# Linear attention on one core: K and V in 8 KB rows over eight heads, a new order of the work, and stores of 2 MB

## The chip, the core and the metric

The kernel runs on one core of a Trainium2 chip. The metric is the time of one execution on the device, in microseconds (us). Of the kernel before, three runs are on record: 126.47, 126.68 and 126.68 us, median 126.68.

## What is computed

Q, K and V have the shape (8, 12, 512, 64) in fp32: 96 heads of 512 rows with 64 columns.

```
Q_feat = max(0, Q) + 1
K_feat = max(0, K) + 1
KV     = K_feat^T V            per head, 64 x 64
K_sum  = sum over rows of K_feat
out    = (Q_feat KV) / (Q_feat K_sum + 1e-10)
```

Each input has 12.58 MB, and so has the output: 50.3 MB cross between HBM and SBUF. Both kernels compute max(x + 1, 1) for the features and leave out the 1e-10.

## The kernel before, in words

**Tiling.** Rows lie on 128 partitions. K and V are loaded with 16 rows (4 KB) to a partition, so a tile of 128 partitions is four heads, 32 partitions to a head. Q is loaded with 32 rows (8 KB) to a partition, the output is stored with 8 rows (2 KB). The work goes in 12 groups g of eight heads (NG = 12). Groups 2s and 2s+1 share their loads: one of K, one of V, one of Q for sixteen heads, 2.1 MB of fp32 each. These go out from GpSimd's queue (POOL) and are cast to bf16 on the way (`load`, L106; `load_q`, L112). The first K alone comes through SP's queue, in fp32 (L93).

**A group.** DVE makes the features of K (`k_features`, two operations at L137). The V rows of each head are copied into their own 64 columns of a wide tile, `v_all` (`v_blocks`): block b holds partitions 32b to 32b+31, in columns 64b to 64b+63, the rest is zero since the start, and four more columns hold ones, one for each head, for K_sum. DVE copies three of the four blocks (L155), ACT the fourth (L153). The first matmul (`keys_values`, L171) multiplies 64 feature columns by 260 columns of `v_all`, 16 for each of two tiles n; n = 0 writes PSUM partitions 0 to 63, n = 1 writes 64 to 127. ACT copies the result into `kva` (L181, L182). Q's features (L137) are transposed on PE (L192, 16 a group) into PSUM, and copied out (L195, mostly ACT). The second matmul (L205) gives numerators and denominators in PSUM, eight matmuls for each of four parts of a group; DVE makes the reciprocal (L222) and the product (L223), called a norm here. `store` writes 1 MB a group (L126, POOL); the last two groups are stored from SP (L129, L132).

**Buffers.** The input pool has two buffers of each tensor, so the loads of pair s+2 wait until the work on pair s has read them. The second matmul's PSUM tiles have two buffers: a part's matmuls wait for the norm two parts back.

**Order.** `tc.manual_schedule()` keeps each engine's instructions in the order in which the program names them, and every engine executes its queue in order. The main loop (L265 to L281) runs over groups:

```
for g in range(last - 1):
    if g % 2:
        transposes(g - 1)
    k_features(g)
    v_blocks(g)
    if g >= 2:
        output(g - 2)
    ...
    keys_values(g)
```

So the output of a group comes two groups after its first matmul. Stores come three groups late (LAG), from POOL, behind the loads of a later pair. The last two groups are written out by hand (L282 to L301).

Of the kernel before, what the change touches and what calls it, by code (L numbers as in the profile page):

```python
# [9 lines left out]
BF16 = mybir.dt.bfloat16  # L10
ALU = mybir.AluOpType

BANK = 512
IN_BUFS = 2
OUT_BUFS = 3
LAG = 3
# [3 lines left out]
def kernel(  # L20
# [10 lines left out]

# [4 lines left out]
    C = 8  # L44
    C2 = 2 * C
    C4 = 4 * C
    R = 4
    NPAIR = B * H * S // (P * C)
    NP = 4
    NG = NPAIR // NP  # L50
# [5 lines left out]

    q_eights = view(Q, C4)
    k_dram = view(K, C2)
    v_dram = view(V, C2)
# [3 lines left out]
    head_pool = ctx.enter_context(tc.tile_pool(name="head_pool", bufs=1))  # L63
    in_pool = ctx.enter_context(tc.tile_pool(name="in_pool", bufs=IN_BUFS))
    kf_pool = ctx.enter_context(tc.tile_pool(name="kf_pool", bufs=2))
    qf_pool = ctx.enter_context(tc.tile_pool(name="qf_pool", bufs=3))
# [8 lines left out]
    NV = 4  # L75
    v_all = const.tile([P, 2, 2, C2, 4 * D1], BF16, name="v_all")
    ones = const.tile([P, 4], BF16, name="ones")
    zero = const.tile([P, 1], FP32, name="zero")
    kva_all = const.tile([P, NV, 4, 2, D1], BF16, name="kva_all")
    kva_diag = [kva_all[:, i] for i in range(NV)]  # L80

    drams = dict(k=k_dram, v=v_dram)
    raw = {}
    bufs = {}
# [4 lines left out]
    cells_of = {}  # L89

    def load_first_k():
        k_raw = head_pool.tile([P, 2, C2, D], FP32, name="k_first")
        nc.sync.dma_start(out=k_raw, in_=k_dram[:, 0:4:2])  # L93
        raw["k", 0] = k_raw

    def load(x, groups):
        s = groups[0] // 2
        if groups[0] % 2 == 0 or (x, s) not in bufs:
            bufs[x, s] = in_pool.tile([P, 4, C2, D], BF16, name=f"{x}_raw")
        if len(groups) == 2:  # L100
            ms = slice(0, 4)
            of = slice(4 * s, 4 * s + 4)
        else:
            ms = slice(groups[0] % 2, 4, 2)
            of = slice(4 * s + groups[0] % 2, 4 * s + 4, 2)
        nc.gpsimd.dma_start(out=bufs[x, s][:, ms], in_=drams[x][:, of])  # L106
        for g in groups:
            raw[x, g] = bufs[x, s][:, g % 2 : 4 : 2]

    def load_q(s):  # L110
        t = in_pool.tile([P, 2, C4, D], BF16, name="q_raw")
        nc.gpsimd.dma_start(out=t, in_=q_eights[:, 2 * s : 2 * s + 2])  # L112
        rows = t.rearrange("p n (r c) d -> p n r c d", c=C)
        for e in range(2):
            raw["q", 2 * s + e] = rows[:, :, :, 4 * e : 4 * e + 4]

    def load_pair(s):
        load("k", (2 * s, 2 * s + 1))
        load("v", (2 * s, 2 * s + 1))
        load_q(s)  # L120

    def store(g):
        s = g // 2
        o_to = o_dram[:, 2 * NP * s : 2 * NP * s + 2 * NP]
        if g < NG - 2:
            nc.gpsimd.dma_start(out=o_to[:, g % 2 : 2 * NP : 2], in_=outs[s][:, g % 2 : 2 * NP : 2])  # L126
            return
        if g == NG - 2:
            nc.sync.dma_start(out=o_to[:, 0 : 2 * NP : 2], in_=outs[s][:, 0 : 2 * NP : 2])  # L129
            return  # L130
        for h in range(2):
            nc.sync.dma_start(  # L132
                out=o_to[:, 2 * h + g % 2 : 2 * NP : NP], in_=outs[s][:, 2 * h + g % 2 : 2 * NP : NP]
            )

    def feature(dst, src):
        nc.vector.tensor_scalar(  # L137
            out=dst, in0=src, scalar1=1.0, scalar2=1.0, op0=ALU.add, op1=ALU.max
        )

    def k_features(g):
        k_raw = raw.pop(("k", g))
        kf = kf_pool.tile([P, C2, 2, D], BF16, name="kf")
        for n in range(2):
            feature(kf[:, :, n], k_raw[:, n])
        kfs[g] = kf

    def v_blocks(g):
        v_raw = raw.pop(("v", g))
        for b in range(4):  # L150
            ps = slice(32 * b, 32 * b + 32)
            if b == 3:
                nc.scalar.copy(out=v_all[ps, g % 2, :, :, b * D : b * D + D], in_=v_raw[ps])  # L153
            else:
                nc.vector.tensor_copy(  # L155
                    out=v_all[ps, g % 2, :, :, b * D : b * D + D], in_=v_raw[ps]
                )

    def q_features(g):
        q_raw = raw.pop(("q", g))  # L160
        qf = qf_pool.tile([P, R, C // 2, 2, D], BF16, name="qf")
        for n in range(2):
            feature(qf[:, :, :, n], q_raw[:, n])
        qfs[g] = qf

    def keys_values(g):
        kf = kfs.pop(g)
        kva_ps = psum_kva.tile([P, 4 * D1], FP32, name="kva_ps")
        for c in range(C2):
            for n in range(2):  # L170
                nc.tensor.matmul(  # L171
                    kva_ps[64 * n : 64 * n + 64],
                    lhsT=kf[:, c, n, :],
                    rhs=v_all[:, g % 2, n, c, :],
                    start=(c == 0),
                    stop=(c == C2 - 1),
                )
        kva = kva_diag[g % NV]
        for n in range(2):
            ps = slice(64 * n, 64 * n + 64)  # L180
            nc.scalar.copy(out=kva[ps, :, n, 0:D], in_=kva_ps[ps, 0 : 4 * D].rearrange("p (b d) -> p b d", b=4))  # L181
            nc.scalar.copy(out=kva[ps, :, n, D], in_=kva_ps[ps, 4 * D : 4 * D1])  # L182

    def transposes(g):
        qf = qfs.pop(g)
        if g % 2 == 0:
            qts[g // 2] = mid_pool.tile([P, C, P, R], BF16, name="qt")
        for half in range(2):
            qt_ps = psum_qt.tile([P, 2, R, P], BF16, name="qt_ps")
            for c in range(2):  # L190
                for r in range(R):
                    nc.tensor.transpose(qt_ps[:, c, r], qf[:, r, 2 * half + c, :, :], identity)  # L192
            copy = nc.vector.tensor_copy if half and g == NG - 2 else nc.scalar.copy
            lo = g % 2 * 4 + 2 * half
            copy(out=qts[g // 2][:, lo : lo + 2], in_=qt_ps.rearrange("p c r q -> p c q r"))  # L195

    def out_matmuls(g, h):
        qt = qts[g // 2]
        kva = kva_diag[(g // 2 * 2 + h) % NV]
        ops = [psum.tile([P, 2, BANK], FP32, tag="ps", name="o_ps") for _ in range(2)]  # L200
        for c in range(C):
            for j in range(2):
                b = 2 * (g % 2) + j
                q = 16 * (4 * h + b)
                nc.tensor.matmul(  # L205
                    ops[c // 4][64 * j : 64 * j + 64, c // 2 % 2, (c % 2) * W : (c % 2) * W + W],
                    lhsT=qt[:, c, q : q + 16, :],
                    rhs=kva[:, b],
                    start=True,
                    stop=True,  # L210
                )
        cells_of[g, h] = ops

    def norms(g, h):
        ops = cells_of.pop((g, h))
        if (g % 2, h) == (0, 0):
            outs[g // 2] = out_pool.tile([P, 2 * NP, C, D], FP32, name="o_sb")
        o_sb = outs[g // 2]
        for i in range(2):
            cells = ops[i][:, :, 0 : 2 * W].rearrange("p b (c n x) -> p b c n x", n=2, x=D1)  # L220
            recip = recip_pool.tile([P, 2, 2, 2, 1], FP32, name="recip")
            nc.vector.reciprocal(out=recip, in_=cells[:, :, :, :, D:D1])  # L222
            nc.vector.tensor_tensor(  # L223
                out=o_sb[:, 2 * h + g % 2 : 2 * NP : NP, 4 * i : 4 * i + 4].rearrange(
                    "p n (b c) d -> p b c n d", b=2
                ),
                in0=cells[:, :, :, :, 0:D],
                in1=recip.to_broadcast([P, 2, 2, 2, D]),
                op=ALU.mult,
            )  # L230

    def output(g):
        for h in range(2):
            out_matmuls(g, h)
            norms(g, h)

    def clear(i):
        t = v_all[:, i].rearrange("p n c x -> p (n c x)").bitcast(FP32)
        w = t.shape[1] * 5 // 8
        nc.vector.memset(t[:, 0:w], 0.0)  # L240
        nc.scalar.copy(out=t[:, w:], in_=zero.to_broadcast([P, t.shape[1] - w]))  # L241
        nc.vector.tensor_copy(
            out=v_all[:, i, :, :, 4 * D : 4 * D1].rearrange("p n c j -> p (n c) j"),
            in_=ones[:, None, :].to_broadcast([P, 2 * C2, 4]),
        )

    with tc.manual_schedule():
        nc.vector.memset(zero, 0.0)
        load_first_k()
        load("v", (0,))  # L250
        load_q(0)
        load("k", (1,))
# [6 lines left out]
        for t in kva_diag:  # L259
            for b in range(4):  # L260
                nc.gpsimd.memset(t[:, b], 0.0)  # L261
# [70 lines left out]
```

## Time and profile before

| | us |
|---|---|
| median of three runs | 126.68 |
| span of the profiled execution, first to last instruction | 124.7 |
| DVE busy | 89.3 (72%) |
| PE busy | 61.8 (50%) |
| ACT busy | 59.6 (48%) |
| POOL busy | 26.1 (21%) |
| mean granted PE clock | 0.847 of full speed |

The profile is of one execution with a span of 124.7 us; its own time beside the span is not recorded, and the three runs lie within 0.21 us of each other. HBM read 37.75 MB and wrote 12.58 MB, 404 GB/s over the span. A load cast from fp32 to bf16 is counted in the slices by the bytes that it writes, half of those that it reads. Matmuls overlap, so a busy time of PE or the mean of one matmul is not its cost; a burst in the timeline, its length by its count, is nearer to that. "PEld" is the weight load.

### The profile page before, as it was taken

How to read it: one execution, taken by the hardware profiler on the slowest of the kernel's cores; microseconds unless marked ns; L12 is line 12 of the kernel's file. 1: busy time of each engine (PE TensorE's matmuls, PEld its weight loads, DVE VectorE, ACT ScalarE, POOL GpSimd, SP SyncE). 2: the span in 40 equal slices, each digit the busy share in tenths (PEclk: the TensorE clock that was granted, in tenths of full speed). 3: DMA queues.
4: the chain of work that ended last, by engine and by line, in shares of the span. 5: the costliest groups of instructions: out<-in, count | busy, mean ns of one | idle time of the engine just before them, and what ended most of it. 6: DMA issues, size and time to landing. Idle time of an engine off the chain costs nothing.

```text
span 124.7 us, 2348 instructions
## 1 busy us (share of the span) xinstructions
PE 61.8 (50%) x960; PEld 50.7 (41%) x960; DVE 89.3 (72%) x191; ACT 59.6 (48%) x86; POOL 26.1 (21%) x51
## 2 busy tenths in 40 slices
PE   0004945200692838539684691069495267775300
PEld 0003735200581827428573490058384155663100
DVE  4895444206999899997999930699959699969700
ACT  7532289306039781956639462601993295450000
POOL 6991023100011630233302420302020200020000
PEclk9999999955589999995999689756999958997555
DMA  3999999999999999999999999999999999999993
GB/s 95 330 214 214 209 198 210 210 214 213 208 213 213 216 214 208 212 213 217 230 405 327 210 212 214 215 338 403 227 212 215 218 255 415 420 413 416 406 409 126
DMA packets 11803, 32.13 MB, mean 258 GB/s; under 512 B 528, under 2 KB 528, under 8 KB 11792
## 3 DMA queue, kind: packets, MB, share of 16 engines
q0 software_dynamic: 10448, 28.84, 97.4%
q1 hardware_dynamic: 1344, 3.15, 6.7%
q8 instruction: 7, 0.11, 0.3%
q14 instruction: 4, 0.03, 0.1%
HBM read 37.75 MB, written 12.58 MB: 404 GB/s over the span
## 4 chain that ended last, share of the span: by engine, by line
DMA 56%; DVE 19%; PE 8%; ACT 6%; issue 3%; POOL 2%; POOLq 0%
DMA v_raw<-in_V_dram 30%; DMA q_raw<-in_Q_dram 26%; DVE o_sb L223 8%; PE kva_ps L171 5%; DVE v_all L155 5%; ACT v_all L153 3%; DVE qf L137 2%; PE qt_ps L192 2%; DVE recip L222 2%; ACT qt L195 2%; POOL v_raw L106 1%; DVE qt L195 1%; ACT kva_all L181 1%; POOL k_raw L106 1%; DVE kf L137 1%
## 5 line engine op out<-in xcount | busy, mean ns | idle before, releaser
L205 PE MATMUL o_ps<-kva_all,qt 128*64 128x130 bf16 x384 | 20.0, 240 | 37.0 <-DVE recip L222 27.0
L171 PE MATMUL kva_ps<-v_all,kf 128*64 128x260 bf16 x384 | 29.8, 320 | 15.8 <-DVE v_all L155 15.6
L155 DVE COPY v_all<-v_raw 32x2048 bf16<-32x2048 bf16 x36 | 25.8, 717 | 13.5 <-DMA v_raw<-in_V_dram 13.1
L223 DVE TENSOR_TENSOR o_sb<-o_ps,recip 128x512 f32<-128x512 f32 x48 | 33.2, 692 | 1.6
L171 PEld LDWEIGHTS <-kf 128*64 128x64 bf16 x384 | 24.6, 130 | 19.0 <-DVE v_all L155 16.0
L205 PEld LDWEIGHTS <-qt 128*64 128x64 bf16 x384 | 14.0, 118 | 42.2 <-issue 26.0
L153 ACT COPY v_all<-v_raw 32x2048 bf16<-32x2048 bf16 x12 | 22.6, 1893 | 16.9 <-DMA v_raw<-in_V_dram 16.7
L195 ACT COPY qt<-qt_ps 128x1024 bf16<-128x1024 bf16 x23 | 22.2, 1015 | 6.8 <-PE qt_ps L192 6.5
L181 ACT CAST kva_all<-kva_ps 64x256 bf16<-64x256 f32 x24 | 8.9, 371 | 27.5 <-PE kva_ps L171 27.3
L126 POOL DMA_DIRECT2D out_dram<-o_sb x10 | 8.6, 864 | 35.9 <-DVE o_sb L223 27.2
L192 PE MATMUL qt_ps<-identity,qf 128*128 128x128 bf16 x192 | 14.8, 235 | 2.0 <-ACT qt L195 1.3
L192 PEld LDWEIGHTS <-qf 128*128 128x128 bf16 x192 | 12.4, 106 | 4.5 <-issue 2.5
L137 DVE TENSOR_SCALAR kf<-k_raw 128x1024 bf16<-128x1024 bf16 x22 | 8.5, 426 | 7.6 <-DMA k_raw<-in_K_dram 7.6
L106 POOL DMA_DIRECT2D k_raw<-in_K_dram x6 | 4.9, 822 | 35.0 <-DVE kf L137 35.0
L222 DVE RECIPROCAL recip<-o_ps 128x8 f32<-128x8 f32 x48 | 9.6, 200 | 1.4 <-PE o_ps L205 1.2
L137 DVE TENSOR_SCALAR qf<-q_raw 128x1024 bf16<-128x1024 bf16 x24 | 8.8, 431 | 2.1 <-DMA q_raw<-in_Q_dram 2.0
L106 POOL DMA_DIRECT2D v_raw<-in_V_dram x7 | 5.4, 766 | 13.4 <-ACT v_all L153 9.3
L240 DVE MEMSET v_all<- 128x2600 f32 x2 | 4.5, 2225 | 0.9 <-issue 0.9
L112 POOL DMA_DIRECT2D q_raw<-in_Q_dram x6 | 4.3, 716 | 0.0
L182 ACT CAST kva_all<-kva_ps 64x4 bf16<-64x4 f32 x24 | 4.1, 170 | 0.0
L241 ACT COPY v_all<-zero 128x1560 f32<-128x1560 f32 x2 | 2.9, 1487 | 0.0
L261 POOL MEMSET kva_all<- 128x130 bf16 x16 | 2.4, 201 | 0.0
(13 smaller groups left out, 5.8 us busy)
## 6 DMA issues: line engine op xcount, KB each, us to landing
out_dram<-o_sb POOLq DMA_DIRECT2D x10, 1024.0 KB, 25.7
q_raw<-in_Q_dram POOLq DMA_DIRECT2D x6, 1024.0 KB, 26.0
k_raw<-in_K_dram POOLq DMA_DIRECT2D x5, 1024.0 KB, 22.1
v_raw<-in_V_dram POOLq DMA_DIRECT2D x5, 1024.0 KB, 23.0
k_first<-in_K_dram SPq DMA_DIRECT2D x1, 1024.0 KB, 4.9
v_raw<-in_V_dram POOLq DMA_DIRECT2D x2, 512.0 KB, 10.7
out_dram<-o_sb SPq DMA_DIRECT2D x1, 1024.0 KB, 7.0
out_dram<-o_sb SPq DMA_DIRECT2D x2, 512.0 KB, 6.4
```

The costliest lines, as they stand in the source:

```text
L106: nc.gpsimd.dma_start(out=bufs[x, s][:, ms], in_=drams[x][:, of])
L126: nc.gpsimd.dma_start(out=o_to[:, g % 2 : 2 * NP : 2], in_=outs[s][:, g % 2 : 2 * NP : 2])
L137: nc.vector.tensor_scalar(out=dst, in0=src, scalar1=1.0, scalar2=1.0, op0=ALU.add, op1=ALU.max)
L153: nc.scalar.copy(out=v_all[ps, g % 2, :, :, b * D : b * D + D], in_=v_raw[ps])
L155: nc.vector.tensor_copy(out=v_all[ps, g % 2, :, :, b * D : b * D + D], in_=v_raw[ps])
L171: nc.tensor.matmul(kva_ps[64 * n : 64 * n + 64], lhsT=kf[:, c, n, :], rhs=v_all[:, g % 2, n, c, :], start=(c == 0), stop=(c == C2 - 1),)
L181: nc.scalar.copy(out=kva[ps, :, n, 0:D], in_=kva_ps[ps, 0 : 4 * D].rearrange("p (b d) -> p b d", b=4))
L192: nc.tensor.transpose(qt_ps[:, c, r], qf[:, r, 2 * half + c, :, :], identity)
L195: copy(out=qts[g // 2][:, lo : lo + 2], in_=qt_ps.rearrange("p c r q -> p c q r"))
L205: nc.tensor.matmul(ops[c // 4][64 * j : 64 * j + 64, c // 2 % 2, (c % 2) * W : (c % 2) * W + W], lhsT=qt[:, c, q : q + 16, :], rhs=kva[:, ...
L222: nc.vector.reciprocal(out=recip, in_=cells[:, :, :, :, D:D1])
L223: nc.vector.tensor_tensor(out=o_sb[:, 2 * h + g % 2 : 2 * NP : NP, 4 * i : 4 * i + 4].rearrange("p n (b c) d -> p b c n d", b=2), in0=cell ...
```

## The change

- **Rows.** K and V come with 32 rows (8 KB) to a partition, as Q did. A tile (n) is then eight heads, an octet, with 16 partitions to a head. Six pairs s of two octets each are worked on (NPAIR = 6).
- **K features.** A block of 32 partitions now holds two heads. DVE writes each octet's K features twice (a = 0, 1): once with the partitions of the odd heads set to zero, once with those of the even. A masked feature is still one operation, max(x + shift, least), with shift and least read per partition from a small tile that `masks()` fills at the start. It covers 128 x 2048 elements.
- **First matmul.** The two halves lie side by side: 128 feature columns by 260 columns of `v_all`, 32 matmuls an octet, all 128 PSUM partitions written. It goes in thirds of 11, 11 and 10, with output parts of the pair before between them.
- **V blocks.** Two of four are made by DVE, two by ACT.
- **Order.** In the pass through pair s: K features and V blocks of octet 0; two output parts of pair s-1, then the thirds of octet 0 with two more parts; K features and V blocks of octet 1; weights (the copies into `kva`) of octet 0; the same for octet 1 and parts 4 to 7; Q features; stores and loads; weights of octet 1; transposes of pair s. In the last pair the Q features come before octet 1's matmuls.
- **Transfers.** The first octet of Q, not K, comes through SP, into a buffer of the output pool. Stores from POOL cover a pair, 2 MB, with `single_packet=True`. Pair 0 is stored ahead of the loads of pair 3; the others behind the last loads. The last pair is stored from SP in parts of 1, 0.5 and 0.5 MB.

The core of the diff:

```diff
-    q_eights = view(Q, C4)
-    k_dram = view(K, C2)
-    v_dram = view(V, C2)
+    q_dram = view(Q, ROWS)
+    k_dram = view(K, ROWS)
+    v_dram = view(V, ROWS)
...
+    def store_pair(s):
+        nc.gpsimd.dma_start(
+            out=o_dram[:, 8 * s : 8 * s + 8], in_=outs.pop(s), single_packet=True
+        )
...
+    def key_value_work(s, n):
+        k_raw = raw.pop(("k", s, n))
+        kf = kf_pool.tile([P, ROWS, 2, D], BF16, name="kf")
+        for a in range(2):
+            nc.vector.tensor_scalar(
+                out=kf[:, :, a],
+                in0=k_raw,
+                scalar1=shift[:, a : a + 1],
+                scalar2=least[:, a : a + 1],
+                op0=ALU.add,
+                op1=ALU.max,
             )
...
+        for b in range(4):
+            ps = slice(32 * b, 32 * b + 32)
+            copy = nc.scalar.copy if b % 2 else nc.vector.tensor_copy
+            copy(out=v_alls[n][ps, :, b * D : b * D + D], in_=v_raw[ps])
...
+    def keys_values(s, n, rows):
+        kf = kfs[s, n]
+        if rows[0] == 0:
+            kva_pss[s, n] = psum_kva.tile([P, 4 * D1], FP32, name="kva_ps")
+        for c in rows:
+            nc.tensor.matmul(
+                kva_pss[s, n],
+                lhsT=kf[:, c].rearrange("p a d -> p (a d)"),
+                rhs=v_alls[n][:, c],
+                start=(c == 0),
+                stop=(c == ROWS - 1),
+            )
...
+    THIRDS = (range(0, 11), range(11, 22), range(22, ROWS))
+
+    def step(s, n):
+
+        parts = range(4 * n, 4 * n + 4) if s else ()
+        for part in parts[:2]:
+            output(s - 1, part)
+        for rows, part in zip(THIRDS, [*parts[2:], None] if s else [None] * 3):
+            keys_values(s, n, rows)
+            if part is not None:
+                output(s - 1, part)
...
+        for s in range(NPAIR):
+            key_value_work(s, 0)
+            step(s, 0)
+            key_value_work(s, 1)
+            weights(s, 0)
+            if s == last:
+                q_features(s)
+            step(s, 1)
+            if s < last:
+                q_features(s)
+            if s == 1:
+                store_pair(0)
+            if s + 2 < NPAIR:
+                load_pair(s + 2)
+            if s + 2 == last:
+                store_pair(1)
+            if s + 2 >= last:
+                store_pair(s - 1)
+            weights(s, 1)
+            for lo in range(0, C, 2):
+                transposes(s, lo)
+        for part in range(8):
+            output(last, part)
```

The functions `weights`, `transposes` and `output` hold the same instructions as before: 4 copies an octet, 32 transposes and 4 copies of 128 x 1024 a pair, and 8 output parts a pair of 8 matmuls, a reciprocal and a product each.

## The prediction

> **What bounds the kernel now.** I read the 40 slices first, then the chain that ended last, then the groups, then the timeline.
>
> ```profile
> DMA  3999999999999999999999999999999999999993
> GB/s 95 330 214 214 209 198 210 210 214 213 208 213 213 216 214 208 212 213 217 230 405 327 210 212 214 215 338 403 227 212 215 218 255 415 420 413 416 406 409 126
> ...
> DMA 56%; DVE 19%; PE 8%; ACT 6%; issue 3%; POOL 2%; POOLq 0%
> ```
>
> The DMA engines are full from the second slice to the last but one, and the chain is mostly DMA. Loads are cast from fp32 to bf16 and counted by the bytes written, so 214 GB/s in a load slice is 428 GB/s read; stores move 405 to 420. So the kernel is bound by its 50.3 MB, and no engine is: DVE, the busiest, has 72% of the span. Per pair of groups (sixteen heads, six such pairs) the transfers take about 20 us, and DVE needs 89.3 / 6 = 14.9 of them. An engine order needing over 20 us a pair would take the bound over. So I price the new order from these groups:
>
> ```profile
> L171 PE MATMUL kva_ps<-v_all,kf 128*64 128x260 bf16 x384 | 29.8, 320 | 15.8 <-DVE v_all L155 15.6
> L155 DVE COPY v_all<-v_raw 32x2048 bf16<-32x2048 bf16 x36 | 25.8, 717 | 13.5 <-DMA v_raw<-in_V_dram 13.1
> L223 DVE TENSOR_TENSOR o_sb<-o_ps,recip 128x512 f32<-128x512 f32 x48 | 33.2, 692 | 1.6
> ...
> L153 ACT COPY v_all<-v_raw 32x2048 bf16<-32x2048 bf16 x12 | 22.6, 1893 | 16.9 <-DMA v_raw<-in_V_dram 16.7
> L195 ACT COPY qt<-qt_ps 128x1024 bf16<-128x1024 bf16 x23 | 22.2, 1015 | 6.8 <-PE qt_ps L192 6.5
> ```
>
> A V block costs ACT 1.89 us and DVE 0.70. Matmuls overlap, so I take them from the timeline, as bursts at full clock (start, length, count at the end):
>
> ```profile
> 90.73 0.42 PE L205 MATMUL o_ps<-kva_all,qt 128*64 128x130 bf16 x8 [0.42 <-DVE o_sb L223]
> ...
> 91.08 1.07 PE L192 MATMUL qt_ps<-identity,qf 128*128 128x128 bf16 x16
> ...
> 91.73 1.93 ACT L195 COPY qt<-qt_ps 128x1024 bf16<-128x1024 bf16 x2
> 92.07 1.71 PEld L171 LDWEIGHTS <-kf 128*64 128x64 bf16 x32
> 92.07 1.98 PE L171 MATMUL kva_ps<-v_all,kf 128*64 128x260 bf16 x32
> ```
>
> Full-width transposes with 128 columns take 1.07 / 16 = 67 ns each; the 64-wide first matmuls take 1.98 / 32 = 62 ns with 260 columns. Twice the columns in less time means that the two halves (n = 0, 1) run side by side: 124 ns a pair.
>
> **The change, part by part.**
>
> *Rows.* K and V join Q at 8 KB rows. Q slices read 2 x 216 GB/s, K/V slices 2 x 211: 24.1 MB of K and V save 1.3 us of transfers. 2 MB stores in single packets have no row: I bound them by the slowest and fastest store slices (405, 420), 0.5 us either way on 10.5 MB, and take 0. All this counts only while DMA is the bound.
>
> *First matmul.* There are still 32 an octet (eight heads), but each is now 128 wide, so nothing runs beside it. Bounds: 62 ns (nothing lost) and 67 x 260 / 128 = 136 ns. I take 124, what a pair took for the same columns and weights: 3.97 us an octet for 1.98, in thirds of 11, 11, 10 (1.36, 1.36, 1.24).
> The Trainium skill (TensorE: Matmul & The Clock Gate, section Back-to-back issue gap) gives 81 ns for streams of N=128 and 131 ns for N=512, by estimate 98 ns at 260. The 67 ns here is already under its 81, so I keep the row; by the page the sum below would be some 6 us shorter.
>
> *V blocks.* ACT makes two of four instead of one: 2 x 1.89 = 3.78 us an octet, 22.7 us more over the kernel; DVE loses one at 0.70.
>
> *K features.* Two 128x2048 operations an octet for two 128x1024, with per-partition scalars, for which there is no row. As a V copy of 2048 (two in 1.38 us) it is 0.69; at the rate of the fp32 first K (128x1024 in 0.78) 1.5; at L223's (512 in 0.692) 2.7 at most. I take 0.69, the row with the same types and length.
>
> *Order.* Here lies the cost. One pass through pair s is, by each engine's program order: ACT copies qt of s-1, then V blocks of octet 0; PE waits with its first third for them; output parts 2 and 3 of s-1 stand behind the first and second third in PE's queue; DVE makes octet 1's K features and V blocks only after the norms of these parts; PE's next thirds wait for those; Q features come after the last norm, transposes after them, and the qt copies after those. So ACT's next V blocks wait for the end of a ring that touches all three engines. Going round:
> - transpose 8 x 0.076 = 0.61, four qt copies at 0.965 = 3.86: 4.47
> - V blocks on ACT, octet 0: 3.78
> - third 1.36, part 0.42, third 1.36, part 0.42, norm 0.84 (reciprocal and multiply, spacing in the timeline): 4.40
> - octet 1 on DVE: 2 x 0.69 + 2 x 0.70 = 2.78 (its ACT blocks are done by then)
> - thirds, parts, norm again: 4.40 (the third third hides behind the last norm and the Q features)
> - Q features, four in 1.43
>
> Sum 21.26, with some ten hand-overs at 0.03 ("issue" in the chain) 21.5 us a pair. DVE (14 us), ACT (13.8), and PE (14) each have room; it is the ring that exceeds 20. In before, output came two groups late, so nothing closed such a ring.
>
> *Start.* Six 1 MB transfers come first. Before, five such landed behind the first (landed at 5.6) by 18.07, 2.5 us each; the fourth of the queue, V of octet 1, lands at 15.6; the second at 10.6. ACT finishes octet 0 at 14.4. Before, the first burst took 3.68 us instead of 1.98: PE starts at half speed. I charge 1.95 us: octet 0's matmuls end at 20.3, octet 1's at 24.3, weights copies (2 x 0.37 + 2 x 0.17, wait 0.1) 25.5, qt copies 29.4.
>
> *Loop and end.* 29.4 + 5 x 21.5 = 136.9 for the last qt copy. Eight norms at 0.84 follow, the first begun just before: last norm 143.3. A last 0.5 MB store alone: 1.25 us of bytes, 2.4 fixed (the 1 MB first load landed in 4.9, 2.5 of it bytes), and 0.6 to the end as now (124.1 to 124.7): span 147.6. Transfers no longer cover this tail.
>
> *Clock.* PE gaps of 2.99 us (before 54.77) and 2.76 (before 69.62) were each followed by a half-clock stretch of 3.4 us. The ring holds one gap of about 3.4 us a pair, while ACT makes V blocks; a half-clock stretch over the following thirds costs up to 1.7 us. Over five pairs that is 0 to 8.5 us; I take the middle, 4.3.
> The Trainium skill (same page, section Part 1: The HAM clock gate) lets the clock fall only after a whole idle window of some 3.4 us. The two rows here show it after shorter gaps, so I don't use that; by the page this term would be near 0, and the time 149.6.
>
> Span 147.6 + 4.3 = 151.9. The profiled execution's span is 124.7 and the median of the runs 126.68, so 2.0 lie around it: **153.9 us**.
>
> POOL: the stores stand in its queue behind the loads (from pair 3 on) and wait for the last norms of the pair before. The store of pair 0 stands ahead of pair 3's loads, which start when it is issued, at about 46, as pair 2's bytes end (18 + 6 x 4.9). Load waits (K 5 behind octet 1's K features of pair 3) cost a few us of DMA, which is no longer the bound. After the last load DMA has only stores and stands idle between them.
>
> **Rivals.**
> 1. *Transfers stay the bound* (other side). If the ring closes in under about 17 us, because the engines' work overlaps across octets more than program order says, all compute fits under the transfers, and the K/V rows decide: 126.7 - 1.3 = 125.4. For: every engine's own work is under 15 us a pair. Against: the trace follows program order on every engine, and even at 62 ns a matmul the ring is 18.8. Chance 0.09; 0.03 more that a smaller gain leaves the time within 0.2%, what a measurement here can't tell from no change.
> 2. *Wide matmuls cost what narrow ones did* (62 ns, or part of the way): the ring loses 4 x 11 x 0.062 = 2.7 us, the start 4: 153.9 - 13.6 - 4, some 137, with 145 for half. For: weight loads and matmuls overlap in rows I can't separate. Against: the 67 ns for 128 columns. Chance 0.13.
> 3. *K features at a lower rate.* At 1.5 us each the ring grows by 2 x 0.8: + 8, 162; at 2.7 by 4: 174. For: no per-partition scalar is in the trace. Against: the types are those of the fast rows. Chance 0.13.
>
> My forecast (146 to 161) has the rest, 0.62. The 8-in-10 range leaves out the fast cases (0.12) and the upper part of rival 3: 138 to 165. Faster 0.09, same 0.03, slower 0.88.
>
> **What would show it.** Right: the chain is ACT, PE and DVE, little DMA; V blocks on ACT 24 at 1.89; first thirds released by ACT's V blocks; the same V block of successive pairs 21 to 23 us apart from pair 1 on; the DMA slices fall below 5 between the stores after about 107 us; 32 first matmuls make 4 us of PE time. Wrong: DMA slices of 9 to the end (rival 1), matmul starts 62 ns apart (2), kf operations above 1 us (3). A ring under 20 us would refute the order argument.

## The result and the profile after

The median of four runs is 160.34 us (159.49 to 161.15) for 126.68 before on the same chip (126.47 to 126.73): the kernel became slower by a factor of 1.264 (95% interval 1.258 to 1.270). The forecast was 153.9, its range 138 to 165. The profiled execution of the changed kernel has a span of 158.4 us, 1.9 less than the median. Here and below, medians and ranges are of all runs, while factors and intervals leave out the runs that were over 1.5% longer than the fastest of their kernel.

From the page of the changed kernel, the granted clock and the DMA engines in 40 slices (3.96 us each), and the chain that ended last, by engine:

```profile
PEclk9999999559879959879959879959999659869955
DMA  5999999999987999999995699999929300006785
GB/s 165 262 211 213 215 212 215 216 215 215 214 172 251 280 208 214 215 214 214 216 214 101 88 212 215 188 247 415 421 110 375 122 0 0 0 4 248 281 325 206
...
PE 38%; ACT 29%; DVE 21%; DMA 5%; issue 2%; ACTq 1%; POOL 0%; POOLq 0%
```

DMA made 56% of the chain before and makes 5% now. Its row has holes from the 22nd slice on, and from some 127 us on it stands idle for four slices. No engine took its place alone: the page gives PE 60% of the span, DVE 59%, ACT 52%. A chain of 88% over three engines, none of which is much more than half busy, is a serial ring. Its parts, in the groups of the same page (count, busy time and mean of one; behind the bar the idle time ahead of them):

```profile
L151 PE MATMUL kva_ps<-v_all,kf 128*128 128x260 bf16 x384 | 61.9, 324 | 42.3 <-ACT v_all L132 32.1
L132 ACT COPY v_all<-v_raw 32x2048 bf16<-32x2048 bf16 x24 | 45.5, 1895 | 7.4 <-DMA v_raw<-in_V_dram 6.8
...
L178 ACT COPY qt<-qt_ps 128x1024 bf16<-128x1024 bf16 x24 | 22.6, 1026 | 0.9 <-PE qt_ps L177 0.8
L119 DVE TENSOR_SCALAR kf<-k_raw,shift,least 128x2048 bf16<-128x2048 bf16 x24 | 18.7, 822 | 3.7 <-DMA k_raw<-in_K_dram 3.6
```

PE waits 32.1 us for ACT's V blocks. ACT itself waits little for DMA (6.8). The mean of 324 ns of a matmul is the length of overlapping records, and says nothing of the rate. The rate is read from bursts.

One turn of the ring, from the first V block of pair 3 on ACT to that of pair 4, as the chain in order of time gives it (start, length, engine, tile, line); reciprocals and norms and the waits of 0.01 to 0.07 us are left out:

```profile
75.77 1.91 ACT v_all L132
...
77.69 1.90 ACT v_all L132
...
79.63 2.54 PE kva_ps L151 x11
82.18 0.57 PE o_ps L188 x8
82.75 1.49 PE kva_ps L151 x11
84.24 0.37 PE o_ps L188 x8
...
85.56 1.44 DVE kf L119 x2
87.01 0.59 DVE v_all L132
...
87.61 0.91 DVE v_all L132
...
88.57 1.40 PE kva_ps L151 x11
89.98 0.57 PE o_ps L188 x8
90.55 2.50 PE kva_ps L151 x11
93.05 0.49 PE o_ps L188 x8
...
94.50 0.68 DVE qf L140 x2
...
95.22 0.64 PE qt_ps L177 x8
...
95.88 2.65 ACT qt L178 x3
...
98.60 1.05 ACT qt L178
...
99.67 1.91 ACT v_all L132
```

23.90 us for one pair. The same V block starts at 28.30, 51.85, 75.77, 99.67 and 121.83, so the turns take 23.55, 23.92, 23.90 and 22.16 us. Each piece starts within 0.1 us of the end of the one before it, and most on another engine. There is no load among the pieces.

Two thirds of eleven matmuls take 2.54 and 2.50 us, another 1.40. Every stretch at half clock in this trace begins and ends on a grid of 3.41 us, and the steps of this grid show why (start and end, length, then busy time and count of PE, PEld, DVE, ACT and POOL, the granted clock, DMA share, GB/s):

```profile
76.21:79.63 3.42, 0.00 (x0) 0.00 (x0) 0.83 (x2) 3.37 (x3) 0.00 (x0) 1.00 1.05 214
79.63:83.04 3.41, 3.41 (x21) 2.14 (x21) 0.21 (x2) 3.38 (x2) 0.00 (x0) 0.50 1.06 214
83.04:86.45 3.41, 3.35 (x45) 2.40 (x42) 2.47 (x5) 0.97 (x4) 0.00 (x0) 1.00 0.64 129
86.45:89.86 3.41, 1.29 (x11) 0.99 (x11) 3.30 (x7) 0.29 (x2) 1.43 (x2) 1.00 0.36 38
89.86:93.28 3.42, 3.42 (x27) 2.20 (x27) 1.36 (x3) 0.00 (x0) 0.00 (x0) 0.50 1.02 199
```

PE is idle through one step and at half clock in the next: that is the gap which the prediction had seen, while ACT makes V blocks. But a step in which PE worked for 1.29 of 3.41 us is followed by half clock as well, so this turn has two half-clock steps and not one. The second follows PE's wait for octet 1's work on DVE, 2.19 us in the timeline (before 88.57). A turn of 23.90 us is seven steps (7 x 3.41 = 23.87), so a turn of this length meets the steps where the one before it did. The turn of 22.16 us has only one half-clock step: there PE waited 1.97 us for DVE and worked for 1.50 us in the step from 110.34 to 113.75, and the next step was at full clock. PE's busy time alone doesn't decide it: the step from 25.02 to 28.43, with 1.93 us of transposes and output matmuls, was followed by half clock.

### The profile page after: what moved, and what is told of

It reads as the page before. It is cut to its first block, busy times and chain, and to the rows that moved or that the text cites. A ratio compares the mean times of both kernels' runs of the same rounds, so it can differ in the third digit from the quotient of the medians.

```text
span 158.4 us, 2335 instructions
## 1 busy us (share of the span) xinstructions
PE 94.6 (60%) x960; PEld 67.0 (42%) x960; DVE 94.1 (59%) x183; ACT 82.8 (52%) x99; POOL 21.6 (14%) x48
## 4 chain that ended last, share of the span: by engine, by line
PE 38%; ACT 29%; DVE 21%; DMA 5%; issue 2%; ACTq 1%; POOL 0%; POOLq 0%
PE kva_ps L151 30%; ACT v_all L132 14%; ACT qt L178 14%; DVE o_sb L198 7%; PE o_ps L188 6%; DMA v_raw<-in_V_dram 5%; DVE kf L119 5%; DVE v_all L132 4%; DVE qf L140 3%; DVE recip L197 2%; PE qt_ps L177 2%; ACT kva L165 1%; ACTq L313 1%; POOL k_raw L93 0%; ACT kva L169 0%
## 5 line engine op out<-in xcount | busy, mean ns | idle before, releaser
L151 PE MATMUL kva_ps<-v_all,kf 128*128 128x260 bf16 x384 | 61.9, 324 | 42.3 <-ACT v_all L132 32.1
L151 PEld LDWEIGHTS <-kf 128*128 128x128 bf16 x384 | 41.3, 113 | 56.6 <-DVE v_all L132 25.1
L132 ACT COPY v_all<-v_raw 32x2048 bf16<-32x2048 bf16 x24 | 45.5, 1895 | 7.4 <-DMA v_raw<-in_V_dram 6.8
L165 ACT CAST kva<-kva_ps 64x256 bf16<-64x256 f32 x24 | 8.9, 371 | 55.4 <-PE kva_ps L151 55.2
L188 PE MATMUL o_ps<-kva,qt 128*64 128x130 bf16 x384 | 22.8, 250 | 7.0 <-ACT qt L178 3.7
L119 DVE TENSOR_SCALAR kf<-k_raw,shift,least 128x2048 bf16<-128x2048 bf16 x24 | 18.7, 822 | 3.7 <-DMA k_raw<-in_K_dram 3.6
L132 DVE COPY v_all<-v_raw 32x2048 bf16<-32x2048 bf16 x24 | 17.7, 737 | 4.2 <-DMA v_raw<-in_V_dram 4.0
L177 PEld LDWEIGHTS <-qf 128*128 128x128 bf16 x192 | 11.4, 97 | 11.2 <-issue 7.8
L106 POOL DMA_DIRECT2D out_dram<-o_sb x5 | 4.9, 982 | 68.7 <-DVE o_sb L198 68.7
L169 ACT CAST kva<-kva_ps 64x4 bf16<-64x4 f32 x24 | 4.0, 168 | 0.0
L257 POOL MEMSET kva<- 128x130 bf16 x16 | 2.4, 207 | 0.0
```

Source lines behind the costliest of these rows:

```text
L106: nc.gpsimd.dma_start(out=o_dram[:, 8 * s : 8 * s + 8], in_=outs.pop(s), single_packet=True)
L119: nc.vector.tensor_scalar(out=kf[:, :, a], in0=k_raw, scalar1=shift[:, a : a + 1], scalar2=least[:, a : a + 1], op0=ALU.add, op1=ALU.max,)
L132: copy(out=v_alls[n][ps, :, b * D : b * D + D], in_=v_raw[ps])
L151: nc.tensor.matmul(kva_pss[s, n], lhsT=kf[:, c].rearrange("p a d -> p (a d)"), rhs=v_alls[n][:, c], start=(c == 0), stop=(c == ROWS - 1),)
L165: nc.scalar.copy(out=kva[po, a::2, n, 0:D], in_=kva_ps[pi, 0 : 4 * D].rearrange("p (b d) -> p b d", b=4),)
L177: nc.tensor.transpose(qt_ps[:, c, r], qfs[s][:, r, lo + c], identity)
```

## The experiments

All kernels start from the changed one, unless another is named. The theory: three engines in program order close a ring in each pair, and the half clock lengthens it. Rivals: PE's time alone, ACT's V blocks alone, or the new transfers set the pace.

**The clock alone.** The tile of the first matmul gets unused columns, and idle matmuls into these keep PE at work ahead of each octet's first third.

```
-            kva_pss[s, n] = psum_kva.tile([P, 4 * D1], FP32, name="kva_ps")
+            kva_pss[s, n] = psum_kva.tile([P, BANK], FP32, name="kva_ps")
+            for _ in range(32 if n == 0 else 20):
+                nc.tensor.matmul(
+                    kva_pss[s, n][:, 4 * D1 : 4 * D1 + P], lhsT=identity, rhs=identity,
+                    start=True, stop=True,
+                )
```

> The changed kernel with 52 idle matmuls a pair (identity by identity, 128 columns, into unused PSUM columns, their result is never read): 32 before the first third of octet 0 and 20 before that of octet 1, where PE waits anyway. They fill PE's gaps and change no result. Clock theory: the granted clock stays at 1.0 from pair 1 on, each third takes 1.4 instead of 2.5 us, the ring falls by about 3 us to 20.8: 143 to 148 us. If the clock is not what lengthened the thirds, or the idle matmuls delay the thirds: 158 to 165.

Measured: 147.76 us (146.42 to 148.48), 1.164 of before (1.157 to 1.171). Work was added, and 12.6 us fell away. The turn from 71.28 on, in the stretches and in the chain of this kernel (its first matmuls stand in line 156):

```profile
71.28:92.13 20.85, 16.19 (x212) 12.58 (x212) 14.36 (x29) 13.10 (x16) 4.09 (x5) 1.00 1.06 211
```

```profile
75.15 1.39 PE kva_ps L156 x11
...
84.30 1.33 PE kva_ps L156 x11
```

The clock is 1.00 for the whole turn, the slow thirds (2.54, 2.50) take 1.39 and 1.33, and the turns take 20.63, 20.85 and 20.85 us. That is the ring without the clock, and it still doesn't go under the transfers' 20 us.

**Half of the first matmul.** Every second of the 32 matmuls of an octet is left out, and with it half of the products of K and V.

```
-        for c in rows:
+        for c in rows[::2]:
...
-                stop=(c == ROWS - 1),
+                stop=(c == ROWS - 2),
...
-    THIRDS = (range(0, 11), range(11, 22), range(22, ROWS))
+    THIRDS = (range(0, 12), range(12, 22), range(22, ROWS))
```

> The changed kernel with every second of the 32 first matmuls of an octet left out (thirds of 6, 5, 5 instead of 11, 11, 10): half of the products of KV are not computed. So PE's first matmuls cost what the narrow pairs of the kernel before cost. Ring theory: 22 of the ring's matmuls fall away, 2.7 us a pair at full clock, 4 where half-clock stretches covered them; V blocks, norms, Q features and qt copies stay: 139 to 147 us, still far above 127. Rival, PE's work is the bound: PE loses a third of its 95 us, 126 to 132.

Measured: 149.25 us (147.21 to 149.36), 1.172 of before (1.163 to 1.180), 2 us over the upper end of what the ring theory gave. PE as the bound would have given 126 to 132; that rival falls. Two thirds in the chain of this kernel show the miss:

```profile
74.30 1.36 PE kva_ps L151 x6
...
81.98 1.48 PE kva_ps L151 x6
```

Six matmuls take what eleven took at full clock: 1.36 / 6 = 227 ns each against 127. With half of its work gone, PE's mean clock falls from 0.859 to 0.775, and all four thirds of the turn run at half clock. They take 5.24 us for 7.93; at full clock it would be about half of the 5.46 of the kernel above.

**V blocks three to one.** ACT makes one of four, as in the kernel before, and DVE three.

```
-            copy = nc.scalar.copy if b % 2 else nc.vector.tensor_copy
+            copy = nc.scalar.copy if b == 3 else nc.vector.tensor_copy
```

> The changed kernel with V blocks shared as before: three on DVE, one on ACT. Ring theory: 1.9 us of ACT leave the ring in octet 0 (DVE's three blocks, 2.1 us, run beside), 0.7 us of DVE come in in octet 1, and PE's gap before octet 0's first third falls from 3.5 to about 1.7 us, under the gap that halves the clock: 149 to 153 us. Rival, ACT's load is the whole cost (45 us of V blocks): nearer to 140. Rival, PE's work is the bound: 158 to 161.

Measured: 150.75 to 156.05 us in four runs, median 153.8. The factor of 1.198 of before (1.187 to 1.208) is of the two shorter runs, 150.75 and 152.88, which lie in what the ring theory gave. So 6 to 9 us come back, much less than with ACT as the bound: ACT is rid of 22.7 us of work. The profile is of one of the longer runs (span 153.0). In its chain the turn from 49.78 to 72.52 has one V block of 1.90 on ACT for two, but a third one of 0.70 on DVE ahead of octet 1, and its thirds take 1.61 to 2.46 us, so a part of them runs at half clock (the first at a mean clock of 0.61). The expectation took PE's shorter gap ahead of octet 0 to be too short for half clock; it is 1.61 us there, and half clock begins half a microsecond into the third.

**Octet 0 of the next pair ahead.** Features and V blocks of the next pair's octet 0 are issued ahead of the weights and transposes of this one, so they leave the ring.

```
+        key_value_work(0, 0)
         for s in range(NPAIR):
-            key_value_work(s, 0)
             step(s, 0)
...
             if s < last:
                 q_features(s)
+                key_value_work(s + 1, 0)
```

> The changed kernel (160.3 us) with one move: K features and V blocks of the next pair's octet 0 stand before the weights copies and transposes of the present pair, so that ACT makes these V blocks ahead of the qt copies. Ring theory: the V blocks of octet 0 (3.8 us) leave the ring, and with them the PE gap of 3.5 us that is followed by one of the two half-clock stretches a pair; the ring goes from 23.9 to about 20 to 21 us, the time to 144 to 149 us. Rival, PE's work is the bound (wide matmuls, 94.6 us busy): the order of ACT's work changes nothing, 158 to 161. Rival, transfers (2 MB stores, loads ahead of stores): 158 to 161.

Measured: 148.97 us (146.0 to 150.2), for 126.8 of before in the same job; with this spread no interval is given. A reordering alone, with the same instructions, brings back 10 to 14 us. V blocks now wait for loads instead: the one at 71.34 waits 10.0 us for V of pair 3.

**Both octets ahead.** To the edit above, octet 1's work comes ahead of octet 0's matmuls and the output parts between them.

```
         for s in range(NPAIR):
+            key_value_work(s, 1)
             step(s, 0)
-            key_value_work(s, 1)
             weights(s, 0)
```

> As the run before, and octet 1's K features and V blocks also stand ahead, before octet 0's matmuls and the norms between them. Ring theory: 3 us of DVE work leave the ring as well, it closes in about 17 to 18 us, near the transfers' own 15 to 20 a pair: 136 to 142 us. Rival, PE's work is the bound: 158 to 161. Rival, transfers: 158 to 161.

Measured: 137.88 us (137.75 to 138.93), 1.090 of before (1.085 to 1.095). Both reorderings together bring back 22.5 us, 8 to 12 of them from this one. What comes last now stands in the chain in order of time:

```profile
45.76 0.70 DVE o_sb L198
...
46.75 0.44 POOL out_dram L106
...
47.92 0.53 POOL k_raw L93
...
48.62 17.98 DMA v_raw<-in_V_dram
...
66.68 1.91 ACT v_all L132
```

The last norm of pair 0 releases its store on POOL, behind the store in POOL's queue stand pair 3's loads, and the V blocks of pair 3 wait for these. With the ring open, the queue order is on the path.

**The store of pair 0 behind the loads of pair 3**, with both octets ahead:

```
-            if s == 1:
-                store_pair(0)
             if s + 2 < NPAIR:
                 load_pair(s + 2)
+            if s == 1:
+                store_pair(0)
```

> The second experiment (both octets ahead, 137.9 us) with the store of pair 0 behind the loads of pair 3 in POOL's queue instead of ahead of them. There the transfers stood at about half between 44 and 50 us, since the loads waited behind a store that waited for the last norm of pair 0, and V of pair 3 landed at 66.7, when DVE and ACT were ready at 63. Theory: with the loads first V of pair 3 lands before they are ready, 3 us are saved: 134 to 136 us. If that store's place doesn't matter: 137 to 138.5.

Measured: 133.41 us (132.91 to 134.18), 1.053 of before (1.048 to 1.057): 4.5 us back, a little more than expected. The V block of pair 3 starts at 59.47 for 66.68.

**Q features ahead as well.** To the kernel above, `q_features(s)` goes ahead of `step(s, 1)` in every pair, so that it isn't behind the norms of its parts.

```
-            if s == last:
-                q_features(s)
+            q_features(s)
             step(s, 1)
             if s < last:
-                q_features(s)
                 key_value_work(s + 1, 0)
```

> As the run before, and the Q features of every pair (not only of the last) stand ahead of octet 1's matmuls and the norms between them, so that transposes don't wait for them. Ring theory: 1 us a pair leaves the ring, which is then shorter than DVE's and PE's own work of 14 to 15 us a pair; what is left above the 126.7 of before is the end, where outputs and the last stores of the last pair follow its last copies uncovered: 130 to 133 us. If the ring was closed already: as the run before.

Measured: 131.85 us (130.79 to 133.32), 1.037 of before (1.032 to 1.042). The slices of its page:

```profile
GB/s 108 321 213 210 218 210 217 215 210 218 214 213 217 210 219 213 213 217 195 394 330 209 220 213 211 220 208 218 218 261 419 420 415 417 160 118 371 200 378 224
```

DMA is full up to the 34th slice (3.26 us each). It loses its pace in the last six slices, where stores wait for norms: it is all but idle from 113 to 116 us and 36% busy from 122 to 124. The last qt copy ends at about 119, eight norms run until 125.7, and the last store comes after them.

**The last pair's transposes ahead**, an attempt on that end: to the kernel above, in the last pair they come ahead of `step(s, 1)`.

```
             q_features(s)
+            if s == last:
+                for lo in range(0, C, 2):
+                    transposes(s, lo)
             step(s, 1)
...
             weights(s, 1)
-            for lo in range(0, C, 2):
-                transposes(s, lo)
+            if s < last:
+                for lo in range(0, C, 2):
+                    transposes(s, lo)
```

> The fastest of the new orders so far (131.85 us), and in the last pair the transposes stand ahead of octet 1's matmuls, so that the four qt copies (3.8 us) don't stand between the last matmul and the last eight norms. Against it, PE waits some 2 us for these copies before octet 1's thirds. If the uncovered end is what is left above 126.7: 128.5 to 130.5. If the whole loop is: 131 to 133.

Measured: 134.53 us (133.23 to 135.26), 1.058 of before (1.053 to 1.063): slower than without it, and outside of both expectations. In the profiled execution (span 131.5 for 130.2) the last norm ends at 125.4, for 125.7 in the kernel above. PE waits for the qt copies ahead of octet 1's matmuls, so these end at 117.16 for 114.63, and most of what is saved behind them is lost ahead of them. The norms of pair 4 between these matmuls also end later, at 116.90 for 114.37, and they release pair 4's store on POOL: it is issued at 117.19 for 114.67. From then on the last 4 MB of stores keep the DMA engines full from about 118.7 to 129.7 us (in the kernel above from 116.2 to 128.8, with the hole at 122 to 124). By this reading of the two traces the late store, and not the last norms, sets the end. It accounts for the 1.3 us between the two spans; the rest of the 2.7 us between the medians stays open. No version tried here beats the kernel before.

**Is ACT's second V block dear by itself?** In the kernel before, ACT makes two of four blocks for one.

```
-            if b == 3:
+            if b % 2:
```

> The kernel before, with V blocks shared as in the change: two on DVE, two on ACT. Ring theory: 22.7 us more on ACT have room where output comes two groups late and transfers are the bound: 126.5 to 127.5. Rival, ACT's load is the cost wherever it stands: 130 or more.

Measured: 127.17 us (126.84 to 127.31), 1.0027 of before (1.0014 to 1.0041). The same 22.7 us more on ACT cost 0.3 to 0.4 us where the transfers cover them. The block isn't dear; its place in the ring is.

**The transfers alone.** Three kernels hold only the loads and stores, in the order of the kernel; all computation is left out, and zeros are stored. One has the transfers of before (K and V in 4 KB rows), one those after (8 KB rows), one those after with this edit in the 2 MB stores:

```
-, single_packet=True
```

> The transfers of the kernel before alone, in the same order and sizes: all features, matmuls and norms are left out, and the stores write zeros. Transfers were its bound, so it should take what the whole kernel takes, less what little the end waited for the last norms: 124.5 to 126.7 us. If compute was the bound of the kernel before: under 120.

> The transfers of the changed kernel alone, in the same order and sizes (8 KB rows, 2 MB stores in single packets), stores of zeros, no other work. The prediction's rows: 1.3 us less than the run before for the rows of K and V, 0.5 either way for the stores: 122.5 to 125.5 us, so that 35 us of the changed kernel's 160 are not transfers. Rival, the changed transfers are themselves what is slow: 150 or more.

> As the run before, with the 2 MB stores in ordinary packets. If single packets are neutral, as the prediction took them: within 0.5 us of it. If they pay for themselves: slower than it by 0.5 to 1.5; if they cost: faster.

Measured: 128.09 us with 4 KB rows (127.69 to 128.73; 1.011 of before, 1.008 to 1.014), 127.57 with 8 KB (127.45 to 127.63; 1.0066, 1.0044 to 1.0087), 127.56 without single packets (127.32 to 127.70; 1.0063, 1.0043 to 1.0084). So the new transfers aren't what makes the kernel slower. The kernel with 8 KB rows is 0.5 us shorter by the medians, with intervals that just overlap; it also differs in the size and order of its stores, so the rows' own share isn't shown. Single packets save nothing that can be seen. Both are above what was expected of them: alone, the transfers take about 1 us more than the whole kernel before, and why isn't settled. Stores there start early, mixed with the loads: with nothing to wait for, the last pair's go out from SP at about 9 us.

## Why the prediction was right

The mechanism was right, and the time 6.4 us too low: one term, the clock, was sized at a third of what it cost, and an error of the other sign hid 2 us of that. Point by point:

1. *The bound moves from DMA to the ring.* Shown, by the chain (56% to 5%) and by the edits: opening the ring for octet 0 and then for octet 1 takes 160.3 to 149.0 (146.0 to 150.2) and 137.9 with the same work. The same work of ACT costs 0.3 to 0.4 us outside the ring (127.17).
2. *The ring without the clock:* 21.5 predicted; 20.63 to 20.85 with PE kept busy. Inside it, transposes and qt copies 4.42 for 4.47, ACT's V blocks 3.82 for 3.78, octet 1 on DVE 3.0 for 2.78 (K features 1.53 for two, where 1.38 were charged), thirds, parts and norm at full clock 4.4 as charged (75.15 to 79.55). Q features are 0.7 for 1.43: only two of the four lie on the chain.
3. *First matmul.* 1.40 / 11 = 127 ns, for 124 taken. Rival 2 (62 ns) falls. The estimate of 98 ns from the Trainium skill (TensorE: Matmul & The Clock Gate, section Back-to-back issue gap) is under what the trace shows for 260 columns at full width.
4. *The start and the end.* The first qt copies ended at 28.29 (29.4 predicted), the last norm is followed by 4.9 us (4.3). Octet 0's first matmuls take 5.5 us (14.46 to 19.98), octet 1's 3.59: 1.9 more, as charged. The granted clock reads 1.00 in both, so the profile shows the slow start but not that it is half clock.
5. *The clock: the term that was mis-sized.* "The ring holds one gap of about 3.4 us a pair" gave 4.3 us in all. It is 12.6 (160.34 to 147.76): 23.9 - 20.85 = 3.05 us a turn, with two half-clock steps for one. The ring holds a second gap, PE's wait of 2.19 us for octet 1's work on DVE. That work stands in the prediction's sum but was not counted as a gap; it is shorter than the 2.76 and 2.99 us of the prediction's rows. The step before this half clock is not idle but 38% busy. Over the loop, from the first V block of pair 1 to that of pair 5, it is 93.53 us for 82.96 with the clock kept, 10.6 in all; the last pass takes 3.7 more, and the kernel with idle matmuls enters the loop 1.5 us later. So the sign "21 to 23 us apart" missed as well: three of four turns are longer. The miss is 12.6 - 4.3 = 8.3, less 2.0 by which the sum without the clock was too long (147.6 for the span of 145.6 that the kept clock gave): 6.3, and 158.4 - 151.9 = 6.5. The Trainium skill (same page, section Part 1: The HAM clock gate) asks for a whole idle window. The trace agrees with it for the step from 76.21 to 79.63, where PE was busy for 0.00 us, and the 38% row speaks against it. By that rule the idle step gives one half-clock step in such a turn, and not a term near 0 as the prediction had read it.
6. *K features at a lower rate* (rival 3): 1.53 us for two in the timeline, 0.765 each, far from that rival's 1.5 each.
7. *Rows 1.3 us, single packets 0.* With the transfers alone, rows and stores together give 0.5, single packets 0.01.
8. *POOL's order.* That the store of pair 0 ahead of pair 3's loads is "no longer the bound" holds in the changed kernel. It cost 4.5 us as soon as the ring was open.

By the medians, the accounts are: 160.3, less 11.4 (octet 0 ahead), 11.1 (octet 1), 4.5 (store behind loads), 1.6 (Q features): 131.9. The runs with octet 0 ahead spread over 4.2 us, so only the sum of the first two, 22.5, is firm. The other 5 us above 126.7 lie by the slices in the uncovered end. That is a reading of the page, and the one edit aimed at it made the kernel slower.

## What to carry to other kernels

Sum the program orders, not the engines: an engine order in which each engine's next work waits for another's last closes a ring, and the time of a turn is the sum around it, however idle each engine is. Move the work of the next turn ahead of the ring's closing wait, and then look again at what the DMA queues hold behind waiting stores. Where PE works in bursts, count the clock's half-speed steps in a first trace before a turn is summed; less work on PE can make what is left slower.

## What the hardware showed unexpectedly

- The half clock follows a step of 3.41 us with PE 38% busy (1.29 us) as well as an idle one, while a step with 44% (1.50 us) was once followed by full clock. Two turns of 23.9 us locked to seven such steps. Idle matmuls of 128 columns, 52 a pair, made the kernel 12.6 us faster.
- With half of the matmuls left out, each of those left took 227 ns in the third shown, for 127.
- The transfers alone (127.57, 128.09) take longer than the kernel that also computes (126.7).
